# Writing the order of four engines by hand ahead of the FFN, and loading projection weights from one queue

## The chip, the cores and the metric

One Trainium2 chip, one core. The metric is the device time in microseconds of one execution of the whole program. A core has five engines that each run their own list of instructions in order: TensorE (PE in the profile: matmuls and transposes; PEld is its weight load), VectorE (DVE), ScalarE (ACT), GpSimd (POOL) and SyncE (SP, which only issues transfers). They wait for each other through semaphores. An instruction that waits holds everything behind it in its own list.

## The reference

One layer of a hybrid encoder for 2048 prompt tokens and 8 x 16 sample tokens, model width 1024, all float32:

```python
n = rmsnorm(x, norm1_g)
z, xbc, dt_raw, q, k, v, f_raw = split_columns(n @ w_in)     # 3088 columns
y_ssd = ssd_mixer(z, causal_dwconv(xbc) ... )                # 8 heads, state 128, conv width 4
y_fox = fox_prompt / fox_sample(q, k, v, logf)               # 8 heads, width 64, forget gates
h = x + concat([y_ssd, y_fox]) @ w_out
y = h + (silu(g) * v) @ w_down,  g, v = causal_dwconv(rmsnorm(h, norm2_g) @ w_up)
```

The final RMSNorm of y is an output, and so are the keys, values, log gates, SSD state and the last rows of both convolutions. The sample tokens attend to 512 cached rows and start from given states.

## The kernel before

Tokens lie in 17 tiles of 128 (16 of the prompt, tile 16 holds the sample tokens). Each float32 operand of a large matmul is split into a high half, rounded to the fast float32 format, and a low half, what is left; a product is three matmuls (`split`, `split2`).

Ahead of the FFN the program has three kinds of work.

- **Projection.** The prompt is taken in four parts of 512 tokens (`NPART`). `a_head(p)` loads the part's inputs transposed (`xT`) and by rows (`xt`), forms the row norms from squares, turns each scale into a diagonal matrix (`dg`), spreads it over the partitions by a matmul with ones, multiplies, and splits the result into `nT`. `a_body(p)` then multiplies by the weights: `proj_tm` with tokens on the partitions (v, gates, z; two halves of a weight tile each), `proj_cm` with columns on the partitions (q, k and the convolution channels). Weights are loaded as `craw` (2 buffers) and split by ScalarE (line 109) and GpSimd (line 112) into `cmw` (3 buffers, `WA`). Consumers of the results are `use_qk`, `use_v`, `use_z` and `use_x`, the last being the convolution: a scaling on ScalarE, three multiply-adds on VectorE, a tanh on ScalarE, a product on VectorE. `gates` computes gate values and cumulative sums.
- **SSD.** `ssd_chunk(c)`, one per tile: loads `xb`, `zt` and the broadcast decay sums `sg`, forms decays with ScalarE, and ends in a transposed tile stored to `mix_d`.
- **Attention.** For each part and head `s_phase` finds row maxima (VectorE, line 671) and `t_phase` forms transposed scores, exponentials `pr` on ScalarE (line 733) and the product with v (`pv`, line 696) two steps later. `sample_attention` does the cached streams.

A loop at the end interleaves them: for each attention step (`u`) it gives out a share of the side work (`sides`: sample attention in part 0, SSD chunks after) and of the filling projection (`fill`, where each piece of a generator says by a credit about how long TensorE takes). Stage 4 of the filling is the output projection: `out_weights` loads and splits `wo`, `out_proj(c)` loads a tile of `mix_d` as `raw`, splits it into `mx` (lines 102, 105) and multiplies.

What sets the order: the loop runs under a manual schedule for TensorE alone, so TensorE's list is the program's order. The lists of VectorE, ScalarE, GpSimd and SyncE are chosen by a planner, which puts instructions where its estimate of their durations has them ready. `DQ = "sass"` says which queue issues a transfer: `dma`, `dS` and `dA` SyncE, `dW` (weights) ScalarE. The FFN follows under the planner: 22 blocks of `up` and `down` in three parts.

## Time and profile before

| | |
|---|---|
| median of 3 runs | 3159.74 us (3157.91 to 3166.94) |
| profiled execution | 3159.18 us, span 3157.5 us |
| TensorE busy | 3039.0 us, 96% of the span |
| VectorE, ScalarE, GpSimd busy | 1788.8, 1066.7, 865.8 us |
| TensorE busy, 0 to 1550 us | 1445.69 us |
| TensorE busy, 1550 to 3157 us (FFN) | 1593.35 us |
| mean granted TensorE clock | 0.984 over the span, 0.97 in 0 to 1550 us |

The span is the profiled execution from its first to its last instruction. In the rows that follow, a stretch of time shows busy microseconds and the number of instructions of each engine, then the granted clock, the mean busy share of the DMA engines and their GB/s; in a timeline row the numbers are the start, the duration, the engine, the line and the operation, and in brackets how long the engine sat idle before it and what it waited for. A matmul that waits for an exponential may wait because ScalarE is held by something else in its list, so the row of the instruction ahead of it has to be read as well.

### The profile page before, as it was taken

The numbers are of one execution on the slowest core, as the hardware profiler recorded it, in microseconds if no ns is written. First come the engines' busy times: TensorE is split into PE (matmuls) and PEld (weight loads), VectorE is DVE, ScalarE is ACT, GpSimd is POOL, SyncE is SP. The second block draws the span as 40 slices with busy tenths as digits, with TensorE's granted clock in tenths as the row PEclk, the third lists the DMA queues.
The fourth block names the chain that finished last, engine by engine and source line by source line (L and its number), as shares of the span: only waits on it lengthen the run. The fifth ranks groups of instructions, "written<-read, shape, count | busy, mean of one in ns | idle before, by whom it ended". The sixth has DMA issues, their size and how long they took to land.

```text
span 3157.5 us, 45849 instructions
## 1 busy us (share of the span) xinstructions
PE 3039.0 (96%) x17888; PEld 2682.1 (85%) x17888; DVE 1788.8 (57%) x3294; ACT 1066.7 (34%) x1927; POOL 865.8 (27%) x654
## 2 busy tenths in 40 slices
PE   7988998899999998999999999999999999999998
PEld 7886877787788775777899999999999999999998
DVE  4264466647565654543455555566555556766666
ACT  3343344444444444332322232233222223332322
POOL 3322322222222212000233232333223232433332
PEclk9998999899999999999999999999999999999999
DMA  4856675575556546445522121232121122322221
GB/s 123 247 174 202 200 244 158 181 223 165 162 155 204 153 132 187 161 148 181 171 67 67 54 69 61 72 116 79 61 67 61 60 67 83 105 67 81 74 69 65
DMA packets 233137, 395.77 MB, mean 125 GB/s; under 512 B 62544, under 2 KB 118488, under 8 KB 232920
## 3 DMA queue, kind: packets, MB, share of 16 engines
q1 hardware_dynamic: 181224, 238.41, 24.3%
q10 hardware_dynamic: 51696, 154.43, 15.8%
q8 instruction: 141, 2.31, 0.3%
q14 instruction: 76, 0.62, 0.1%
HBM read 314.51 MB, written 78.25 MB: 124 GB/s over the span
## 4 chain that ended last, share of the span: by engine, by line
PE 85%; DMA 8%; DVE 2%; ACT 2%; issue 1%; SPq 1%; POOL 1%; ACTq 0%; DVEq 0%; POOLq 0%
PE mm L120 11%; PE mm L121 11%; PE mm L122 11%; PE pv L696 6%; PE dn L1025 5%; PE dn L1026 5%; PE dn L1027 5%; PE mm L444 3%; PE mm L445 3%; PE mm L446 3%; DMA xt<-in_xr 2%; PE dn L923 2%; PE dn L925 2%; PE dn L924 2%; PE mm L397 2%; PE mm L399 2%
## 5 line engine op out<-in xcount | busy, mean ns | idle before, releaser
L105 POOL TENSOR_TENSOR wr<-raw,wr 128x1024 fp32r<-128x1024 f32 x198 | 476.5, 2415 | 1032.5 <-ACT wr L102 1024.5
L120 PE MATMUL mm<-nT,wr 128*128 128x386 f32 (+1 forms) x2112 | 696.4, 330 | 1.3 <-ACT wr L102 0.8
L121 PE MATMUL mm<-nT,wr 128*128 128x386 f32 (+1 forms) x2112 | 695.3, 329 | 0.1
L122 PE MATMUL mm<-nT,wr 128*128 128x386 f32 (+1 forms) x2112 | 694.4, 329 | 0.0
L1003 DVE SCALAR_TENSOR_TENSOR ac<-mm,cw,ac 128x384 f32<-128x384 f32 (+1 forms) x528 | 301.6, 571 | 344.8 <-ACT ac L1001 337.1
L1001 ACT ACTIVATE ac<-mm,cw 128x384 f32<-128x384 f32 (+1 forms) x264 | 172.7, 654 | 784.6 <-PE mm L122 784.0
L1028 DVE TENSOR_TENSOR y<-y,dn 128x512 f32<-128x512 f32 x374 | 255.0, 684 | 267.4 <-PE dn L1027 264.6
L121 PEld LDWEIGHTS mm<-nT,wr 128*128 128x128 f32 x2112 | 399.3, 189 | 6.8 <-DVE nT L105 0.3
L120 PEld LDWEIGHTS mm<-nT,wr 128*128 128x128 f32 x2112 | 397.5, 188 | 7.7 <-ACT wr L102 1.1
L122 PEld LDWEIGHTS mm<-nT,wr 128*128 128x128 f32 x2112 | 397.9, 188 | 5.7
L112 POOL TENSOR_TENSOR cmw<-craw,cmw 128x512 fp32r<-128x512 f32 (+1 forms) x192 | 248.6, 1317 | 467.8 <-ACT cmw L109 348.1
L444 PE MATMUL mm<-nT,cmw 128*128 128x256 f32 (+2 forms) x1024 | 309.7, 302 | 12.7 <-DVE cac L489 8.6
L671 DVE TENSOR_REDUCE nm<-s 128x1 f32<-128x512 f32 (+2 forms) x320 | 192.9, 607 | 198.6 <-PE s L668 114.1
L445 PE MATMUL mm<-nT,cmw 128*128 128x256 f32 (+2 forms) x1024 | 299.0, 292 | 0.0
L446 PE MATMUL mm<-nT,cmw 128*128 128x256 f32 (+2 forms) x1024 | 299.0, 292 | 0.0
L1025 PE MATMUL dn<-wr,ht 128*128 128x512 f32 x748 | 294.4, 394 | 2.9 <-DVE y L1028 1.7
L696 PE MATMUL pv<-pr,v 128*128 128x512 f32 (+3 forms) x640 | 293.5, 549 | 0.5 <-issue 0.5
L1026 PE MATMUL dn<-wr,ht 128*128 128x512 f32 x748 | 292.7, 391 | 0.0
L1027 PE MATMUL dn<-wr,ht 128*128 128x512 f32 x748 | 290.1, 391 | 0.0
L102 ACT CAST wr<-raw 128x1024 fp32r<-128x1024 f32 x198 | 203.2, 1042 | 174.1 <-PE dn L1027 161.4
L733 ACT ACTIVATE pr<-s 128x512 f32<-128x512 f32 (+1 forms) x320 | 169.3, 531 | 237.3 <-PE s L729 173.2
L668 PE MATMUL s<-ks,q 68*128 68x512 f32 (+2 forms) x320 | 199.8, 630 | 20.0 <-ACT pr L733 11.2
(294 smaller groups left out, 5174.9 us busy)
## 6 DMA issues: line engine op xcount, KB each, us to landing
raw<-in_w_up ACTq DMA_DIRECT2D x132, 512.0 KB
raw<-in_w_down ACTq DMA_DIRECT2D x66, 512.0 KB
craw<-in_w_cm ACTq DMA_DIRECT2D x64, 512.0 KB
k<-k_d SPq DMA_DIRECT2D x80, 256.0 KB
craw<-in_w_tm ACTq DMA_DIRECT2D x24, 512.0 KB
q_d<-qk SPq DMA_DIRECT2D x96, 128.0 KB
k_d<-qk SPq DMA_DIRECT2D x96, 128.0 KB
ks<-k_d SPq DMA_DIRECT2D x80, 136.0 KB
```

What stands on the lines that cost most here:

```text
L105: leng.tensor_sub(lo, src, hi.bitcast(F32))
L120: T.matmul(ps[:, :W], whi(k), wt[:, 0, k, :W], start=k == 0, stop=False)
L121: T.matmul(ps[:, :W], whi(k), wt[:, 1, k, :W], start=False, stop=False)
L122: T.matmul(ps[:, :W], wlo(k), wt[:, 0, k, :W], start=False, stop=k == n - 1)
L444: T.matmul(ps[:, :W], wc[:, 0, k, :], wk[:, 0], start=k == 0, stop=False)
L445: T.matmul(ps[:, :W], wc[:, 0, k, :], wk[:, 1], start=False, stop=False)
L446: T.matmul(ps[:, :W], wc[:, 1, k, :], wk[:, 0], start=False, stop=k == KT - 1)
L696: m = T.matmul(pv[:, of:512], vr[:, jj], pr[:, :512 - of], start=first, stop=last)
L1003: V.scalar_tensor_tensor(ac[:, 0:n], ps[:, j:j + n], cw2[:, ct, j:j + 1], ac[:, 0:n], op0=ALU.mult, op1=ALU.add)
L1025: T.matmul(ps, ht[:, 0, ts_], wd[:, 0, cc], start=x == 0, stop=False)
L1026: T.matmul(ps, ht[:, 0, ts_], wd[:, 1, cc], start=False, stop=False)
L1027: T.matmul(ps, ht[:, 1, ts_], wd[:, 0, cc], start=False, stop=x == len(g) - 1)
```

## The change

Between the start of the attention loop's program and the FFN, the manual schedule now covers TensorE, VectorE, ScalarE and GpSimd: each runs in the order in which the program writes its instructions. SyncE keeps the planner, and so does what is written ahead of that block (the first two steps of the first head) and the FFN. With that:

- Weight tiles of the projection come from one list, `queue_of_weights`; `wload` issues from SyncE, `wsplit` splits, and `pump`, called after every piece of projection, splits the next tile when one of the three buffers is free and keeps up to two loaded. The order of projections changes: convolution tiles alternate with z, and q of the first pair stands ahead of v's first half.
- In `a_head`, the row squares are spread out, one per two pieces, each load one step ahead of its use; for the first part the diagonals go to VectorE, the low halves too, and squares lie in `k12` buffers.
- `gates`, `ssd_chunk` and `sample_attention` get more steps between a load and its use, and `sides` gives chunks out differently (7 to 15 in the last part).
- `out_weights` splits both halves on GpSimd and no longer waits for the last exponential; `out_rows` loads a tile of mixed rows ahead of the projection before it and splits it inside.

The core of the diff:

```diff
-            sq = at([P, 2, 4, 256], "cmw", WA)
+            sq = []
             for kk in range(2):
-                S.activation(sq[:, kk, :, :n * P], xTs[kk][:, :, :n * P], AF.Square)
+                sq.append(bt_([P, 4 * 264], "k12", KB)[:, 0:D].rearrange("p (k t) -> p k t", k=4))
+                S.activation(sq[kk][:, :, :n * P], xTs[kk][:, :, :n * P], AF.Square)
...
                 dg = at([P, P], "dg", 2)
-                S.activation(dg, ident, AF.Identity, scale=x)
+                if first:
+                    V.tensor_scalar_mul(dg, ident, x)
+                else:
+                    S.activation(dg, ident, AF.Identity, scale=x)
...
                 split(xT[:, :, :N], wt[:, 0, kk:kk + 4, col:col + N], wt[:, 1, kk:kk + 4, col:col + N], S,
-                      V if kk else G)
+                      V if kk or first else G)
...
         xTs = load(*todo[0])
-        ss = [sizes(todo[0][2] + c) for c in range(4)]
-        yield
+        xt = half_row(0)
+        yield
+        ss = []
+        for n in range(8):
+            if n % 2 == 0:
+                x = at([P, 2], "ss", 4)
+            S.activation(xt, xt, AF.Square, accum_out=x[:, n % 2:n % 2 + 1])
+            if n < 7:
+                xt = half_row(n + 1)
+            if n % 2:
+                V.tensor_add(x[:, 0:1], x[:, 0:1], x[:, 1:2])
+                rsq(x[:, 0:1], D)
+                ss.append(x[:, 0:1])
+            yield
...
+    def wload():
+        src, n = wq[len(raws)]
+        raw = at([P, 4 * 272], "craw", 2)
+        raw = raw[:, 0:D].rearrange("p (k c) -> p k c", c=P) if n is None else raw[:, 0:4 * n].rearrange("p (k c) -> p k c", c=n)
+        dma(raw, src.rearrange("p (k c) -> p k c", c=P) if n is None else src)
+        raws.append(raw)
+
+    def wsplit():
+        j = len(tiles)
+        n = wq[j][1]
+        if n is None:
+            we = at([P, 2, KT, P], "cmw", WA, F32R)
+        else:
+            we = at([P, 2, 4, n], "cmw", WA, F32R)
+        split2(raws[j], we[:, 0], we[:, 1], G)
+        tiles.append(we)
+
+    def pump():
+
+        if len(tiles) < len(raws) and len(tiles) - used[0] < WA:
+            wsplit()
+        while len(raws) < len(wq) and len(raws) - len(tiles) < 2:
+            wload()
...
-        for ct in range(8):
-            yield from proj_cm(8 + ct, use_x(ct), PAD1)
-        yield from proj_tm(i["w_tm"][1], 256, use_z(0))
-        yield from proj_tm(i["w_tm"][2], 256, use_z(1))
+        yield from proj_cm(use_x(0), PAD1)
+        yield from proj_tm(256, use_z(0))
+        yield from proj_cm(use_x(1), PAD1)
+        yield from proj_tm(256, use_z(1))
+        for ct in range(2, 8):
+            yield from proj_cm(use_x(ct), PAD1)
...
         dma(sg.rearrange("p h l -> p (h l)"), ac_d[c:c + 1].rearrange("c h p -> c (h p)").to_broadcast([P, D]))
+        yield
+        yield
...
             w = op.tile([P, 2, D], F32R, tag="wo", name="wo", bufs=KT)
-            with tc.issue_after(exps[-1]):
-                split2(raws[k], w[:, 0], w[:, 1], G)
+            split(raws[k], w[:, 0], w[:, 1], G, G)
...
+    def out_rows(c):
+
         mr = op.tile([P, KT, P], F32, tag="raw", name="raw", bufs=2)
+
+        parts = [slice(0, KT - 1), slice(KT - 1, KT)] if 12 <= c < 16 else [slice(0, KT)]
+        for ks in parts:
+            dA(mr[:, ks], mix_d[c][:, ks])
+        yield
         mx = op.tile([P, 2, KT, P], F32R, tag="mx", name="mx", bufs=2)
-
-        for ks in ([slice(0, KT - 1), slice(KT - 1, KT)] if 12 <= c < 16 else [slice(0, KT)]):
-            dA(mr[:, ks], mix_d[c][:, ks])
+        for ks in parts:
             split(mr[:, ks], mx[:, 0, ks], mx[:, 1, ks], S, V)
+        yield mx
...
-            if k in (12, 40) and hd:
+            if hd and (k >= 8 and k % 2 == 0 and k <= 24 or k == 40):
                 next(hd)
...
-    sides = {0: (sample_attention, 5 * NB + 1), 1: (lambda: chunks(SMP, 0, 1, 2), 49), 2: (lambda: chunks(3, 4, 5, 6, 7), 51),
-             3: (lambda: chunks(*range(8, 16)), 81)}
-
-    with tc.manual_schedule(engines={nc.tensor.engine}):
+    sides = {0: (sample_attention, 6 * NB + 1), 1: (lambda: chunks(SMP, 0, 1), 45), 2: (lambda: chunks(2, 3, 4, 5, 6), 61),
+             3: (lambda: chunks(*range(7, 16)), 109)}
+
+    with tc.manual_schedule(engines={e.engine for e in (T, V, S, G)}):
```

Three places show what moves. First, ScalarE's list near the end of part 0's q and k projections and the start of the convolution. `xt` are the half rows that are squared for the next part, `cac` and `cth` the convolution before and in its tanh, `ev` is evicted z or v, `craw` and `cmw` are the raw and split weights. Before:

```order
L197 ACTIVATE xt,ss<-xt 128x512
L487 ACTIVATE cac<-mm,cw_169 128x384
L109 CAST cmw<-craw 128x1024
L197 ACTIVATE xt,ss<-xt 128x512
L487 ACTIVATE cac<-mm,cw_169 128x256
L432 DMA craw<-in_w_cm 128x1024
L497 ACTIVATE cth<-cac 128x384
L197 ACTIVATE xt,ss<-xt 128x512
L497 ACTIVATE cth<-cac 128x256
```

And with the change:

```order
L484 ACTIVATE ev<-mm 128x256
L259 ACTIVATE xt,ss<-xt 128x512
L109 CAST cmw<-craw 128x1024
L541 ACTIVATE cac<-mm,cw_182 128x256
L551 ACTIVATE cth<-cac 128x256
L109 CAST cmw<-craw 128x1024
L803 ACTIVATE pr<-s 128x512
L259 ACTIVATE xt,ss<-xt 128x512
L541 ACTIVATE cac<-mm,cw_182 128x384
L551 ACTIVATE cth<-cac 128x384
```

The squares now stand mostly among z's evictions, the weight load has left the list, and each tanh follows its scaling directly, where before another instruction stood between.

Second, ScalarE's list where the output projection begins under attention (`wo` the output weights, `mx` a tile of mixed rows, `sg` a chunk's decays, `pr` exponentials). Before:

```order
L109 CAST wo<-raw 128x1024
L733 ACTIVATE pr<-s 128x512 x3
L109 CAST wo<-raw 128x1024
L102 CAST mx<-raw 128x1024
L733 ACTIVATE pr<-s 128x512 x2
L532 ACTIVATE sg<-sg,acs 128x128 x8
L102 CAST mx<-raw 128x1024
L533 ACTIVATE sg<-sg 128x1024
```

And with the change:

```order
L803 ACTIVATE pr<-s 128x512 x2
L602 ACTIVATE sg<-sg,acs 128x128 x8
L603 ACTIVATE sg<-sg 128x1024
L803 ACTIVATE pr<-s 128x512 x2
L612 COPY bs<-s 128x256
L803 ACTIVATE pr<-s 128x512 x2
L102 CAST mx<-raw 128x1024 x2
L803 ACTIVATE pr<-s 128x512
```

The casts of `wo` are gone from ScalarE (GpSimd has them), and the exponentials no longer stand behind them.

Third, SyncE's list in part 0, around the first z tiles of the change (`xb_d` and `z_d` are stores of the convolution and of z, `ks` a load for attention). With the change:

```order
L421 DMA craw<-in_w_tm 128x1024
L554 DMA xb_d<-cth 128x2x128
L699 DMA ks<-k_d 68x512
L554 DMA xb_d<-cth 128x2x128
L556 DMA xb_d<-cth 128x128
L487 DMA z_d<-ev 128x256 x2
L421 DMA craw<-in_w_tm 128x1024
L195 DMA xt<-in_xr 128x512
```

Before, no `craw` stood in this list: the loads were ScalarE's, as in the first piece above. Now they stand between stores that wait for ScalarE's and VectorE's results.

More of the change, by code (lines that the diff above doesn't have):

```diff
@@ L185, in sizes_by_columns @@
                 for k in range(KT):
-                    T.matmul(pz[:, c:c + 1], sq[:, k // 4, k % 4, c * P:(c + 1) * P], ones[:, 0:1], start=k == 0, stop=k == KT - 1)
+                    T.matmul(pz[:, c:c + 1], sq[k // 4][:, k % 4, c * P:(c + 1) * P], ones[:, 0:1], start=k == 0, stop=k == KT - 1)
             ss = at([P, 2], "ss", 4)
@@ L403, in proj_tm @@
                     yield 1.45
+            used[0] += 2
         dtf = at([P, 5, 16], "dtf", 1)
@@ L423, in use_z, with proj_cm @@
             return f
-        yield from proj_tm(i["w_tm0"], 272, use_v(1))
-        gs = gates(p, dtf)
-        next(gs)
-        yield from proj_tm(i["w_tm"][0], 256, use_v(0))
-        def load_cm(ct):
-            raw = at([P, 4 * 272], "craw", 2)
-            dW(raw[:, 0:D], i["w_cm"][ct])
-            wc = at([P, 2, KT, P], "cmw", WA, F32R)
-            split2(raw[:, 0:D].rearrange("p (k c) -> p k c", c=P), wc[:, 0], wc[:, 1], G)
-            return wc
-        def proj_cm(ct, use, pad):
-            wc = load_cm(ct)
+        def proj_cm(use, pad):
+            wc, = need(1)
             for w, wt in wins:
@@ L450, in proj_cm @@
                 yield W * 0.0055
+            used[0] += 1
         def use_qk(kind, pair):
@@ L887, in hybrid_step @@
     tp = op = pso = None
-    wo = []
+    wo, ready = [], []
     def out_weights():
@@ L937, in out_proj @@
                             yield 1.36
+                        if e and k == 4 and nxt is not None:
+                            ready.append(next(nxt))
         for e in range(2):
@@ L1201, in out_steps @@
         yield from out_weights()
-        for c in [SMP] + list(range(11)):
-            yield from out_proj(c)
+        cs = [SMP] + list(range(11))
+        g = out_rows(cs[0])
+        next(g)
+        yield ("wait", 3)
+        mx = next(g)
+        for n, c in enumerate(cs):
+            g = out_rows(cs[n + 1]) if n + 1 < len(cs) else None
+            if g:
+                next(g)
+            yield from out_proj(c, None, mx, g)
+            mx = ready.pop() if g else None
     F = ExitStack()
```

82 lines of the change are left out of this document (59 added, 23 removed).

## The prediction

> **What bounds the kernel now.** I read the table by stretches first (length, busy time of each engine, granted TensorE clock, DMA share), cut where the work changes: head, projections alone, four stretches of attention mixed with projections and SSD chunks, output projection under attention, FFN.
>
> ```profile
> 0.00:50.00 50.00, 30.77 (x153) 29.77 (x154) 22.61 (x67) 17.37 (x24) 19.74 (x28) 0.97 0.37 118
> 50.00:160.00 110.00, 102.45 (x725) 99.06 (x725) 39.57 (x118) 33.98 (x80) 35.19 (x31) 1.00 0.72 218
> 160.00:480.00 320.00, 285.28 (x2240) 244.82 (x2239) 169.01 (x438) 120.83 (x265) 87.75 (x84) 0.92 0.65 200
> 480.00:800.00 320.00, 303.96 (x2046) 254.02 (x2046) 199.91 (x398) 136.71 (x295) 87.91 (x92) 0.97 0.61 183
> 800.00:1180.00 380.00, 368.44 (x2382) 296.42 (x2380) 222.05 (x422) 163.30 (x343) 91.97 (x100) 0.99 0.54 162
> 1180.00:1250.00 70.00, 55.14 (x259) 36.87 (x260) 35.76 (x57) 32.80 (x64) 25.79 (x28) 0.88 0.66 194
> 1250.00:1550.00 300.00, 299.66 (x1406) 226.32 (x1405) 134.60 (x206) 92.85 (x189) 19.57 (x43) 1.00 0.48 164
> 1550.00:3157.00 1607.00, 1593.35 (x8689) 1494.83 (x8687) 965.26 (x1589) 468.81 (x669) 497.89 (x250) 1.00 0.23 74
> ```
>
> TensorE sets the time; the FFN (1607 us) is full and untouched. Ahead of it TensorE idles 19.2 + 7.6 + 34.7 + 16.0 + 11.6 + 14.9 + 0.3 = 104.3 us. Length times (1 - clock) adds 1.5 + 25.6 + 9.6 + 3.8 + 8.4 = 48.9 us of withheld clock. No other engine is over two thirds busy in a stretch. So the prize is small gaps, and the next views say what ends them: TensorE's waits, then ScalarE's, both for 0 to 1550 us (total, times, longest).
>
> ```profile
> PE s L570 <- ACT pr L733: 12.6, 2, 9.1
> PE s L668 <- ACT pr L733: 11.2, 6, 5.1
> PE mm L444 <- DVE cac L489: 8.6, 3, 5.0
> PE s L588 <- DVE ss L198: 7.8, 1, 7.8
> ACT xt L197 <- DMA xt<-in_xr: 64.7, 21, 6.3
> ACT mx L102 <- PE dn L925: 60.8, 15, 9.8
> ACT cth L497 <- DVE cac L489: 39.2, 31, 4.0
> ACT sg L532 <- DMA sg<-ac_d: 35.0, 14, 5.7
> ```
>
> TensorE waits for softmax exponentials (pr) that are not slow themselves: they stand in ScalarE's queue behind an instruction that waits for a transfer (xt, sg, mx). The timeline of ScalarE and TensorE shows the largest such gap:
>
> ```profile
> 1230.82 1.04 ACT L109 CAST wo<-raw 128x1024 fp32r<-128x1024 f32 x1 [6.43 <-DMA raw<-in_w_out]
> 1236.57 1.04 ACT L102 CAST mx<-raw 128x1024 fp32r<-128x1024 f32 x1 [4.71 <-DMA raw<-mix_d]
> 1237.52 1.08 ACT L733 ACTIVATE pr<-s 128x512 f32<-128x512 f32 x2
> 1238.16 2.08 PE L570 MATMUL s<-sst,xb 128*128 128x256 f32 x4 [9.06 <-ACT pr L733]
> ```
>
> **The change, part by part.** The matmuls stay the same in number and kind; only waits can move.
>
> Head. The row-norm diagonals move from ScalarE to VectorE, and both low halves of the first windows go to VectorE.
>
> ```profile
> 16.77 0.71 POOL L189 TENSOR_TENSOR ss<-ss,mhalf 128x2 f32<-128x2 f32 x1 [1.53 <-DVE ss L188]
> 19.56 0.69 ACT L206 ACTIVATE dg<-ident,ss 128x128 f32<-128x128 f32 x2 [1.17 <-DMA q_d<-q]
> 20.02 1.22 PE L225 MATMUL tp<-dg,ones 128*128 128x128 f32 x4 [5.79 <-ACT dg L206]
> 26.49 0.59 PE L399 MATMUL mm<-cmw,nT 128*128 128x272 f32 x1 [1.61 <-POOL nT L105]
> ```
>
> The scale is ready at 17.48 and ScalarE takes it at 19.56; VectorE can take it at once: 2 us. Two more diagonals follow later; with the GpSimd wait I take -3 us (0 to -5).
>
> Weight loads: 96 leave ScalarE's queue for SP's. ScalarE loses issue time that is on no path. Where TensorE has only projections (50 to 160 us) the 12 constant-row stores now fall too, since their fill is in VectorE's program order; before, SP did them in the head:
>
> ```profile
> 10.17 6.52 SPq L1162 DMA_DIRECT2D q_d<-q  x8
> 17.11 6.89 SPq L1162 DMA_DIRECT2D k_d<-q  x4
> ```
>
> That is 13.8 us of SP's queue, ahead of the v stores that free the eviction buffers. Three buffers and three PSUM tiles stand between; I take 0, with bounds -4 (half of the 7.6 us idle) and +10.
>
> Squares of the next part's rows (24 of xt). They were bunched, each load issued once the square before it was done; now they are two projection steps apart, with the load issued a step ahead. Stretch 160:480 holds the first eight and the sample attention, whose caches are now loaded a step ahead too. Of its 34.7 us idle I take half, -17, because the two projection steps there are short against a load and some waits stay (bounds 0 and -28).
>
> Stretch 480:800. The one long gap is VectorE's bunch, in its timeline, with TensorE's row behind it:
>
> ```profile
> 544.08 3.39 DVE L713 RECIPROCAL rdb<-rdb 128x128 f32<-128x128 f32 x4 [0.76 <-ACT rdb L710]
> 550.21 3.09 DVE L229 SCALAR_TENSOR_TENSOR xT<-xT,g1c,tp 128x256 f32<-128x256 f32 x8
> 553.22 2.55 DVE L717 TENSOR_TENSOR yl<-yl,rdb 128x512 f32<-128x512 f32 x1
> 557.13 2.07 PE L588 MATMUL s<-k,cm 128*128 128x256 f32 x4 [7.85 <-DVE ss L198]
> ```
>
> In written order one reciprocal goes to each attention step and the four multiplies stand apart: -8 of 16.0 (bounds 0, -13). Stretch 800:1180: chunk loads get two more steps before use, which is the sg wait: -5 of 11.6 (0 to -9).
>
> Stretch 1180:1250. Output weights are split wholly on GpSimd, so ScalarE no longer waits for them, and the mixed rows are loaded a tile ahead.
>
> ```profile
> L112 POOL TENSOR_TENSOR wo<-raw,wo 128x512 fp32r<-128x512 f32 x16 | 20.2, 1282 | 24.8 <-ACT wo L109 24.3 <-DMA k<-k_d 0.4
> L109 ACT CAST wo<-raw 128x1024 fp32r<-128x1024 f32 x8 | 8.3, 1040 | 13.7 <-DMA raw<-in_w_out 13.7
> ```
>
> GpSimd's cast of such a tile has no row: between ScalarE's 1.04 us and GpSimd's own subtraction, 2.56; I take 2.56, the same engine. Eight add 20.5 us to 25.8 busy of 70, so it fits; the v fills and the chunk norms queue behind up to 5 us. -11 of 14.9 (-5 to -13).
>
> Idle removed: 3 + 17 + 8 + 5 + 11 = 44 us.
>
> Clock. The withheld time goes with the gaps in its stretch: 25.6 x 17/34.7 + 9.6 x 8/16 + 3.8 x 5/11.6 + 8.4 x 11/14.9 = 25 us. TensorE was not busy all through a slow slice:
>
> ```profile
> 280.00:300.00 20.00, 13.93 (x81) 8.15 (x84) 8.01 (x23) 8.67 (x21) 2.93 (x4) 0.67 0.59 185
> 860.00:880.00 20.00, 19.77 (x116) 15.88 (x115) 13.38 (x23) 7.86 (x15) 3.02 (x3) 0.92 0.47 155
> 858.96 0.50 PE L729 MATMUL s<-q,k 68*128 68x512 f32 x1 [2.43 <-DVE q L686]
> ```
>
> 13.93 of 20 is 0.70, so -17 us (0 to -34).
>
> The Trainium skill ("TensorE: Matmul & The Clock Gate", Part 1) says that the clock halves after an idle window of about 3.4 us and is full again after as long a busy one. The second and third rows do not bear out a single gap as the condition: the clock fell to 0.92 right after a gap of 2.43 us. By the page, with every longer gap gone, all the clock returns; that is the first rival.
>
> New cost. In the convolution the order now is ScalarE's scale, three VectorE steps, ScalarE's tanh, with nothing between.
>
> ```profile
> L489 DVE SCALAR_TENSOR_TENSOR cac<-mm,cw,cac 128x256 f32<-128x256 f32 x192 | 91.8, 479 | 60.9 <-ACT cac L487 58.3
> ```
>
> ScalarE is held 3 x 0.479 = 1.44 us in each of 64 windows, 92 us, against 39 now: +53 us of hold. Today 8.6 of those 39 us reach TensorE, a share of 0.22: +12 us (0 to +53).
>
> **Sum.** -44 - 17 + 12 = -49. From the profiled execution's own 3159.2 us (span 3157.5; the median of the runs, 3159.7, is the same) this gives **3110 us**. Its own range: half of what is removed, -30 + 12, gives 3141; gaps nearly gone, 65 of idle and 25 of clock with no new cost, gives 3069.
>
> **Rivals.**
>
> First, the clock pays in full: the gaps that are left are too short or too few to slow it. -44 - 0.70 x 48.9 + 12 = -66, 3093 us. For it: 1250:1550 runs at 1.00 with 0.3 us idle. Against: the 2.43 us gap above.
>
> Second, the conv hold reaches TensorE whole: -44 - 17 + 53 = -8, 3151 us, within the noise. For it: VectorE is 60% busy in 480:800, so three steps rarely start at once. Against: exponentials are used two attention steps after they are issued.
>
> Third, slower: SP is now the only queue for weights, and its order is still the planner's. A load behind a store waits for that store's data.
>
> ```profile
> 236.45 13.05 SPq L422 DMA_DIRECT2D z_d<-ev  x5
> 177.91 5.03 DMA craw<-in_w_cm
> L109 ACT CAST cmw<-craw 128x1024 fp32r<-128x1024 f32 (+1 forms) x96 | 100.1, 1044 | 18.0 <-PE mm L399 18.0
> L112 POOL TENSOR_TENSOR cmw<-craw,cmw 128x512 fp32r<-128x512 f32 (+1 forms) x192 | 248.6, 1317 | 467.8 <-ACT cmw L109 348.1 <-issue 34.5 <-DMA k<-k_d 21.2
> ```
>
> Five z stores held SP for 13 us. A load caught behind them, 13 late, lands after 5 and is split in 1.0 + 2.6; a tile lasts 1120 / 96 = 11.7 us (96 loads by about 1120 us), so some 10 us reach TensorE. Five such loads undo the gain; ten, spread over the four parts, make it 3159 - 49 + 100 = 3210 us. For it: stores of z and of the convolution are interleaved tile by tile with the loads. Against: the ring keeps two raw and three split tiles, and ScalarE's own queue, where loads stood till now, was held as long by xt and mx.
>
> The Trainium skill ("DMA: Bandwidth & Descriptors", section "Issuing engines are not separate DMA queues") says that all issuers share the same 16 DMA engines, so a second one saves only issue time. By it the move costs nothing; it leaves out that a waiting store holds its queue, as the 13.05 us row shows.
>
> **Chances.** Forecast 0.55, first rival 0.13, second 0.12, third 0.20. The likeliest case alone spans 3069 to 3141 us. For 8 in 10 I take 3062 to 3185: below are a few hundredths of the first case and rival one, above about two thirds of the third. A measurement here tells 0.3%, 9.5 us. Faster: 0.55 + 0.13 + a little of the second = 0.69; same 0.10; slower 0.21.
>
> **What will show it.** Right: in 160:480 TensorE busy by 300 of 320 us at the same work and clock at 0.96 or more; no exponential behind mx, wo or sg; xt's 64.7 us down by more than half; the FFN stretch unchanged at 1607 us. Wrong: matmuls of the projections waiting for a cmw split whose load left SP late (third), ScalarE's tanh waits over 90 us with TensorE behind them (second), or a head longer than 50 us to the same matmul. The forecast fails if the idle ahead of the FFN stays above 85 us.

## The result, and the profile after

The change makes the kernel slower: 3231.39 us (median of 4 runs, 3228.09 to 3234.06) against 3161.38 us (3157.91 to 3166.94), a ratio of 1.0228 with a 95% interval of 1.0213 to 1.0243. The forecast was 3110 us; the third rival had the sign but, as will be seen, not the cause.

The profiled execution has a span of 3227.8 us against 3157.5. TensorE's busy time grew from 3039.0 to 3065.5 us at the same 17888 matmuls: 26.5 us. That goes with a lower granted clock, 0.976 over the span against 0.984. Its idle time (span less busy) grew from 118.5 to 162.3 us: 43.8. Together 70.3, the whole difference.

The first view is the table by stretches of the kernel after, cut where the prediction cut it, with the stretch before the FFN (at 1627 us now) apart; three rows between 1180 and 1627 us are left out. Columns: window, length, busy time of TensorE, its weight loads, VectorE, ScalarE and GpSimd with their instructions, granted clock, DMA share, GB/s.

```profile
0.00:50.00 50.00, 30.07 (x134) 29.06 (x135) 20.85 (x54) 14.45 (x16) 11.87 (x20) 0.90 0.34 117
50.00:160.00 110.00, 93.64 (x634) 91.85 (x634) 27.87 (x92) 26.68 (x60) 27.94 (x22) 0.89 0.58 170
160.00:480.00 320.00, 269.77 (x2054) 232.10 (x2052) 142.49 (x412) 102.59 (x220) 76.68 (x74) 0.90 0.60 181
480.00:800.00 320.00, 294.53 (x1955) 244.70 (x1955) 182.45 (x377) 125.94 (x271) 86.81 (x89) 0.95 0.62 183
800.00:1180.00 380.00, 365.09 (x2373) 293.55 (x2372) 225.08 (x430) 168.16 (x357) 101.88 (x111) 0.99 0.58 168
...
1627.00:3228.00 1601.00, 1588.07 (x8666) 1490.63 (x8665) 964.38 (x1587) 466.44 (x667) 495.77 (x249) 1.00 0.23 73
```

The FFN takes 1601 us as it did. All is lost ahead of it, and by the clock column mostly before 480 us: the stretch from 50 to 160 us had a clock of 1.00 and has 0.89.

Since the work in a fixed window differs between the two kernels, the timelines were also lined up by work: the start of the n-th first score matmul of the attention (line 728 before, 798 after; 320 of them in each). This table is counted from TensorE's timeline; the four kernels at the right are experiments that follow.

| attention step | before | after | TensorE alone | VectorE free | spaced | spaced, VectorE free |
|---|---|---|---|---|---|---|
| 0 | 168.2 | 184.1 | 178.0 | 172.7 | 188.1 | 173.8 |
| 8 | 261.5 | 282.6 | 260.5 | 260.3 | 282.7 | 257.7 |
| 24 | 413.6 | 452.1 | 413.3 | 408.8 | 444.6 | 406.4 |
| 32 | 454.1 | 510.7 | 467.2 | 467.5 | 498.0 | 458.1 |
| 64 | 608.7 | 667.5 | 615.5 | 624.9 | 655.6 | 609.1 |
| 128 | 846.4 | 900.9 | 848.3 | 860.1 | 881.8 | 836.1 |
| 248 | 1223.1 | 1290.3 | 1238.4 | 1237.8 | 1266.3 | 1211.7 |
| 256 | 1269.5 | 1326.4 | 1274.7 | 1272.1 | 1304.7 | 1246.0 |
| 319 (last) | 1461.2 | 1521.1 | 1471.5 | 1466.8 | 1499.0 | 1441.0 |

After minus before is +15.9 us when attention begins, +56.6 at step 32, and about that at the last step (+59.9). Most of the loss is made in the first part: head, gates, and the sample attention among the first part's projections. From there to the last step the change loses and gains about as much: 10.6 us lost from step 32 to 248, 10.3 gained from 248 to 256. The remaining 10.4 of the 70.3 us come between the last step and the FFN, where TensorE has one hole of 4.18 us up to 1550.21 (it waits for VectorE's addition into y, line 1023) and a clock of 0.97 against 1.00; a part of that stretch is work that stood ahead of the last step before.

Two holes of TensorE show how. The first is in the stretch with projections alone. These rows are from the timelines of SyncE, VectorE and TensorE after, with other rows between them left out:

```profile
72.00 8.04 SPq L1245 DMA_DIRECT2D q_d<-q  x8
80.09 5.25 SPq L1245 DMA_DIRECT2D k_d<-q  x4
91.90 0.27 SPq L355 DMA_DIRECT2D k_d<-g_2k  x1
80.76 0.68 DVE L354 COPY g_2k<-tp 8x512 f32<-8x512 f32 x1 [0.55 <-PE tp L352]
94.66 0.68 DVE L354 COPY g_2k<-tp 8x512 f32<-8x512 f32 x1 [13.22 <-DMA k_d<-g_2k]
95.26 0.20 DVE L361 TENSOR_TENSOR g_dm<-g_ld,blkb 128x64 f32<-128x64 f32 x1
95.61 0.66 PE L363 MATMUL tp<-g_dm,ones 128*128 128x64 f32 x2 [13.05 <-DVE g_dm L361]
```

VectorE has filled a one-buffer row (g_2k) at 81.4 us and must fill it again. The store that frees it is issued by SyncE at 91.90 only, behind the twelve constant rows and what piled up behind them. VectorE stands, and g_dm, a 0.20 us product whose inputs were there at 70.8 us, stands behind it in the list; TensorE waits 13.05 us for that product, and its clock is 0.62 from 80 to 100 us.

The second is at the end of the first part:

```profile
429.30 0.40 SPq L788 DMA_DIRECT2D mix_d<-yl  x1
434.06 0.58 ACT L779 COPY yl<-pv 64x512 f32<-64x512 f32 x1 [12.30 <-DMA mix_d<-yl]
436.32 0.16 DVE L925 TENSOR_TENSOR snm<-snm 128x1 f32<-128x1 f32 x1 [12.94 <-ACT pr L924]
437.01 0.42 DVE L515 SCALAR_TENSOR_TENSOR qk<-mm,qk 128x256 fp32r<-128x256 f32 x1
437.90 0.59 PE L497 MATMUL mm<-nT,cmw 128*128 128x260 f32 x1 [8.98 <-ACT ev L518]
```

A late store holds ScalarE's copy of yl; the sample attention's exponentials (pr, line 924) stand behind that copy; VectorE's sum of them (snm) waits 12.94 us; the eviction of a projection (qk, line 515) stands behind the sum; the eviction of ScalarE behind it frees the PSUM tile for which TensorE waits 8.98 us. ScalarE, VectorE and TensorE each stood at the head of their list for the one before.

### The profile page after: what moved, and what is told of

Same layout as the page of the kernel before. It is cut to its first block, busy times and chain, and to the rows that moved or that the text cites. A ratio compares the mean times of both kernels' runs of the same rounds, so it can differ in the third digit from the quotient of the medians.

```text
span 3227.8 us, 45891 instructions
## 1 busy us (share of the span) xinstructions
PE 3065.5 (95%) x17888; PEld 2696.5 (84%) x17888; DVE 1784.4 (55%) x3302; ACT 1056.0 (33%) x1914; POOL 863.3 (27%) x651
## 3 DMA queue, kind: packets, MB, share of 16 engines
q10 hardware_dynamic: 28656, 103.83, 10.3%
## 4 chain that ended last, share of the span: by engine, by line
PE 77%; DVE 5%; DMA 5%; ACT 2%; issue 2%; SPq 1%; POOL 0%; DVEq 0%; ACTq 0%; POOLq 0%
PE mm L120 11%; PE mm L121 11%; PE mm L122 11%; PE pv L766 5%; PE dn L1108 5%; PE dn L1109 5%; PE dn L1110 5%; PE mm L497 2%; PE mm L499 2%; PE mm L498 2%; PE dn L1004 2%; PE dn L1006 2%; PE dn L1005 2%; PE s L799 1%; PE s L798 1%
```

## The experiments

Two theories at the start. **Q**: SyncE, now the only queue for the weights, is late with loads and stores. **O**: VectorE, ScalarE and GpSimd in written order stand still at the head of their lists, where the planner had put other work ahead. The runs were made in five rounds, and the median of the kernel before moved between 3156.32 and 3162.40 us from round to round, so a few microseconds between runs tell nothing; each ratio is to the kernel before in the same round.

**TensorE alone by hand** (`te_only`)

```diff
-    with tc.manual_schedule(engines={e.engine for e in (T, V, S, G)}):
+    with tc.manual_schedule(engines={nc.tensor.engine}):
```

> The order of ahead-of-FFN work is kept by hand for TensorE alone; ScalarE, VectorE and GpSimd go back to the planner's order, and everything else of the change (loads, stores, queues) stays. Theory Q (one queue: weight loads, constant rows and late stores on one list make the loss): the loss stays, 3210 to 3230 us. Theory O (order: ScalarE, VectorE and GpSimd stand still at the head of a hand-written list, where the planner put other work ahead): the loss goes, 3165 us or less.

Measured: 3177.89 us (3172.93 to 3180.18), ratio 1.0056 (1.0037 to 1.0076). With the loads, stores and queues of the change in place, 53 of 70 us are gone: O carries most, though not all that it promised (3165). The rest, some 16 us, is the cost of everything else in the change; 10 us of it are there at the start of the attention.

**Constant rows early** (`const_early`)

```diff
+    constant_rows()
     with tc.manual_schedule(engines={e.engine for e in (T, V, S, G)}):
...
-            if k == 12:
-                constant_rows()
```

> The constant rows' stores are issued in the head, before the hand-written order begins. Theory Q: the 13.05 us hole of TensorE at 82.56 goes, and with it the cold clock behind it, so 15 to 20 us less than the change, about 3213. Theory O: under 8 us less, because another wait of the list takes its place, about 3225.

Measured: 3233.6 us, ratio 1.0231 (1.0201 to 1.0260). No gain, and both numbers for it were off. From ScalarE's and TensorE's timelines of that run:

```profile
28.64 1.06 ACT L183 ACTIVATE k<-qk 128x1024 f32<-128x1024 f32 x1 [18.13 <-DMA qk<-in_xTw]
33.01 0.59 PE L461 MATMUL mm<-cmw,nT 128*128 128x272 f32 x1 [14.69 <-ACT nT L102]
98.62 0.66 PE L363 MATMUL tp<-g_dm,ones 128*128 128x64 f32 x2 [4.95 <-DVE g_dm L361]
```

The hole did shrink, from 13.05 to 4.95 us, and a new one of 14.69 us stands in the head (2.83 us there in the change): SyncE issues the second window's load at 22.92, behind the rows, ScalarE stands 18.13 us for it, and the split of the first window (nT), for which TensorE waits, stands behind that in ScalarE's list. It moved.

**Weights from ScalarE's queue** (`act_queue`, and `te_only_act_queue` with TensorE alone by hand)

```diff
-        dma(raw, src.rearrange("p (k c) -> p k c", c=P) if n is None else src)
+        dW(raw, src.rearrange("p (k c) -> p k c", c=P) if n is None else src)
```

> The projection weights are issued from ScalarE's queue instead of SP's; the order is that of the change. Theory Q: SP's list is shorter by all weight loads, at least 30 us less than the change, 3200 or less. Theory O: within 10 us of 3231, the weights were there in time on either queue.

Measured: 3345.07 us, ratio 1.0583 (1.0553 to 1.0614). Neither theory had this: 114 us more. ScalarE's timeline of the run, beside one load:

```profile
278.93 1.03 ACT L109 CAST cmw<-craw 128x1024 fp32r<-128x1024 f32 x1
282.60 0.33 ACTq L421 DMA_DIRECT2D craw<-in_w_tm  x1
282.98 0.56 ACT L541 ACTIVATE cac<-mm,cw 128x256 f32<-128x256 f32 x1 [3.03 <-POOL cmw L112]
```

The load needs the buffer that ScalarE has just cast at 278.93 and that GpSimd's subtraction still reads. In written order ScalarE waits for that, 3 us here, before it can issue, and the convolution behind it waits too. So the issue of a load is an instruction with a wait, and it holds what is behind it. Counted over the whole timeline, ScalarE stands idle for 284 us directly ahead of the 96 issues here, and for 75 us in `te_only_act_queue`, where the planner orders its list. The Trainium skill ("DMA: Bandwidth & Descriptors", section "Issuing engines are not separate DMA queues") says that issuing from several engines at once saves the issue time alone; here the choice of the engine was worth 114 us in one order of the list and under 8 in the other:

> TensorE alone in written order (3178 us), and the weight loads issued from ScalarE's queue as before the change, instead of SP's. If SP as the only queue costs by itself (my third rival), at least 8 us come back, 3170 or less. If not, 3174 to 3184; with all four by hand the same edit cost 114 us, which would then belong to ScalarE's written order.

Measured: 3170.35 us (3168.48 to 3171.98), ratio 1.0030 (1.0014 to 1.0046), where `te_only` had 1.0056 (1.0037 to 1.0076). The intervals overlap; it is 7 us lower by the medians, at the edge of what was expected of Q, and about a tenth of the loss at the most.

**A buffer for the late store** (`yl_apart`) and **the sums later** (`sums_later`) each take one link out of the second hole's chain.

```diff
-            vn = bt_([NT, 512], "yl", 2)
+            vn = bt_([NT, 512], "xe", 1)
```

> The sample attention's v rows are held in another buffer (that of xe), so that the copy into yl on ScalarE does not wait for SP's store of the v rows. If ScalarE's 12.30 us and 7 us holds by that store are on the path, attention steps 0 to 32 take 10 to 15 us less than in the change, about 3218. If the gates on VectorE or the conv's tanh are late next, the time stays within 4 us of 3231.

```diff
-            V.tensor_add(nm[:, 5:6], nm[:, 3:4], nm[:, 4:5])
-            V.reciprocal(nm[:, 5:6], nm[:, 5:6])
-            V.tensor_scalar_mul(nm[:, 6:8], par, nm[:, 5:6])
             yield
...
             V.tensor_copy(pt5, pk[0:NT, 0:P])
             yield
+            V.tensor_add(nm[:, 5:6], nm[:, 3:4], nm[:, 4:5])
+            V.reciprocal(nm[:, 5:6], nm[:, 5:6])
+            V.tensor_scalar_mul(nm[:, 6:8], par, nm[:, 5:6])
```

> The change, with one thing moved: in the sample attention VectorE's three small steps on the exponentials' sums stand two pieces later in its list, behind the transposes' copy, so that VectorE no longer waits there for ScalarE's exponentials (26.7 us in 8 waits between 180 and 520 us in the change, longest 12.9). Theory V (VectorE's list, held by ScalarE's results, is what costs in the first part): attention steps 0 to 32 get 8 to 15 us shorter, 3216 to 3223 us. If the hold comes from the projection's evictions instead: within 5 us of 3231.

Measured: 3226.24 us, ratio 1.0207 (1.0178 to 1.0237), and 3233.02 us, ratio 1.0231 (1.0201 to 1.0261). The first took the 8.98 us hole away and was 8 us ahead of the change at step 24, of which 4 were left at step 40: 5 us at the end by the medians, half of what I expected, and the intervals of the two overlap, so a gain in time is not shown. The second gave nothing, and the timeline of VectorE says why:

```profile
437.62 0.42 DVE L515 SCALAR_TENSOR_TENSOR qk<-mm,qk 128x256 fp32r<-128x256 f32 x1 [13.64 <-ACT qk L514]
```

The next instruction of the list took the wait over: it reads ScalarE's result too, and ScalarE stood as long as ever (12.73 us for yl).

**Where and on which engine** (`hand_late`, `vector_free`, `scalar_free`)

```diff
-    with tc.manual_schedule(engines={e.engine for e in (T, V, S, G)}):
+    with tc.manual_schedule(engines={e.engine for e in (T,)}):              # hand_late: to step 40, then all four
+    with tc.manual_schedule(engines={e.engine for e in (T, S, G)}):         # vector_free
+    with tc.manual_schedule(engines={e.engine for e in (T, V, G)}):         # scalar_free
```

> TensorE alone in written order up to attention step 40 (projection of the first part and the sample attention), all four engines in written order from there to the FFN. With all four by hand 69 us were lost, with TensorE alone 16. Theory O1: the other engines' written order costs only in the first part, where sample attention, projection and gates meet; then 3175 to 3185 us. Rival O2: it costs wherever it is used, and what came late in the first part only covers it later; then 3200 us or more.

> TensorE, ScalarE and GpSimd in written order, VectorE by the planner. If VectorE's list is what holds the others (the convolution's steps, the gates, the row maxima), most of the 53 us between the change and TensorE alone returns: 3195 us or less. If ScalarE's list is it (exponentials behind tanh, copies and scalings that wait), it stays above 3215 us.

> TensorE, VectorE and GpSimd in written order, ScalarE by the planner. TensorE's gaps in the change end mostly on ScalarE (exponentials pr), so if ScalarE's list is the cause, 3195 us or less; if VectorE's list holds what ScalarE waits for, above 3215 us. If neither this nor the run with VectorE free falls under 3200, the two hold each other.

Measured:

| | us | ratio to before |
|---|---|---|
| hand_late | 3181.57 (3179.68 to 3185.46) | 1.0066 (1.0043 to 1.0089) |
| vector_free | 3168.97 (3161.57 to 3173.21) | 1.0027 (1.0013 to 1.0041) |
| scalar_free | 3251.30 (3250.72 to 3251.88) | 1.0279 (1.0249 to 1.0309) |

So O1 holds by the times: with four engines by hand from step 40 on, no difference from TensorE alone can be told (1.0066 against 1.0056). The two profiles also reach the last step together (1472.2 and 1471.5 us); only from there to the FFN's first matmul does `hand_late` take longer, 103.4 us against 97.3. That stretch takes 103 to 104 us in the change, `spaced` and `scalar_free` too, and 97 to 98 in `vector_free` and `spaced_vector_free`, so some 6 us are lost there wherever VectorE is by hand. And the order that costs most is VectorE's: with it alone given back to the planner 62 us return. Giving back ScalarE's alone makes it 20 us slower still, the one result of the three that I had no account of beforehand: ScalarE's list then differs, but what it reads still comes from VectorE in written order.

What the planner does with VectorE shows at the first hole. From SyncE's and VectorE's timelines of `vector_free` (the first and the last row of the constant rows' twelve stores, then VectorE; rows between are left out):

```profile
10.04 3.68 SPq L1245 DMA_DIRECT2D q_d<-q  x6
24.76 1.01 SPq L1245 DMA_DIRECT2D k_d<-q  x1
68.11 0.22 DVE L361 TENSOR_TENSOR g_dm<-g_ld,blkb 128x64 f32<-128x64 f32 x1
75.27 0.68 DVE L354 COPY g_2k<-tp 8x512 f32<-8x512 f32 x1 [1.56 <-PE tp L352]
78.89 0.67 DVE L354 COPY g_2k<-tp 8x512 f32<-8x512 f32 x1
```

The fill of the constant rows is an instruction of VectorE; the planner pulls it into the head, so the stores fall at 10 to 26 us, where before they fell at 10 to 24. And it takes g_dm at 68.11, 10.8 us ahead of the second copy of g_2k behind which it was written.

**Each step behind the result it reads** (`spaced`, and `spaced_vector_free` with VectorE by the planner). The projections' evictions become generators that a list holds; each goes one step on at every half piece of projection:

```diff
                 S.activation(ac[:, :off], ps[:, PAD1:W], AF.Identity, scale=cw1[:, ct, 3:4], bias=cw1[:, ct, 4:5])
-                for j in range(3):
-                    V.scalar_tensor_tensor(ac[:, 0:n], ...)
-                S.activation(th[:, :off], ac[:, :off], AF.Tanh)
-                V.scalar_tensor_tensor(th[:, :off], ...)
+                def g():
+                    for j in range(3):
+                        V.scalar_tensor_tensor(ac[:, 0:n], ...)
+                    yield False
+                    S.activation(th[:, :off], ac[:, :off], AF.Tanh)
+                    yield False
+                    V.scalar_tensor_tensor(th[:, :off], ...)
+                    yield True
+                owed.append(g())
```

The same for the second step of z and of q and k; the sums stand as in `sums_later`.

> The same, and in the projection's evictions (q and k, z, convolution) each engine's step stands half a projection piece or more behind the step of the other engine whose result it reads; all four engines are still in written order. Theory V: the waits of VectorE and ScalarE on each other (33.7, 27.2, 26.7, 17.6 us on VectorE; 20.6 and 18.3 on ScalarE between 180 and 520 us) go, and with them half or more of the 62 us between the change and VectorE by the planner: 3200 us or less. If written order as such costs (each list waits for something else next): above 3215 us.

> The same spacing, VectorE by the planner, the others in written order: 3169 us without the spacing. My prediction took 12 us of TensorE's time (0 to 53) for ScalarE's hold by the convolution's tanh. If that holds, 3150 to 3160 us; if the hold reaches TensorE whole, 3120 to 3140; if it reaches nothing, 3165 to 3172.

Measured: `spaced` 3204.82 us, ratio 1.0142 (1.0112 to 1.0171); `spaced_vector_free` 3144.22 us (3142.49 to 3145.36), ratio 0.9958 (0.9936 to 0.9981). By the medians, the spacing gives 27 us beside VectorE's written order (5 us short of what theory V asked) and 25 beside a free VectorE: the two add. The 3144 us lie between the two ranges that I gave for that run, and the kernel is faster than both that were compared, than the one before by 0.4%, with an interval that ends below 1. Its table by stretches, cut at the start of the attention, step 32, the last step and the FFN, and below it that of before, cut at the same work:

```profile
0.00:174.00 174.00, 146.91 (x956) 143.85 (x957) 64.80 (x193) 49.10 (x96) 45.72 (x49) 0.94 0.57 171
174.00:458.00 284.00, 254.71 (x2021) 217.61 (x2021) 150.53 (x395) 101.90 (x223) 80.74 (x77) 0.92 0.67 205
458.00:1441.00 983.00, 952.94 (x5798) 750.54 (x5797) 569.23 (x1065) 408.61 (x881) 234.74 (x264) 0.98 0.58 172
1441.00:1540.00 99.00, 98.22 (x454) 80.56 (x453) 43.95 (x64) 25.82 (x50) 7.70 (x14) 1.00 0.64 216
```

```profile
0.00:168.00 168.00, 141.22 (x930) 136.44 (x931) 66.49 (x199) 55.27 (x111) 58.21 (x62) 0.99 0.61 186
168.00:454.00 286.00, 256.46 (x2049) 218.98 (x2048) 151.02 (x402) 106.07 (x233) 78.27 (x75) 0.92 0.67 206
454.00:1461.00 1007.00, 959.02 (x5813) 758.56 (x5813) 568.33 (x1050) 413.98 (x868) 225.77 (x255) 0.97 0.55 167
1461.00:1556.00 95.00, 94.22 (x437) 77.40 (x436) 38.97 (x59) 24.88 (x49) 8.23 (x14) 1.00 0.57 204
```

Head and end still lose 6 and 4 us; the third row gains 24, 18 of it idle (48.0 to 30.1) and 6 busy. That is the size of the gain that the prediction looked for from 480 to 1250 us, once VectorE's list is the planner's and the evictions are spaced. In the stretch from which it took most, 160 to 480 us, the second row gains 2.

**Is it ScalarE's and GpSimd's written order that gains there?** (`spaced_te_only`, `spaced_te_act_queue`: the spacing with TensorE alone by hand, weights from SyncE or ScalarE)

> The spacing with TensorE alone in written order; VectorE, ScalarE and GpSimd by the planner. Without the spacing this was 3178 us, and with the spacing and VectorE alone free 3144. If the planner undoes or has no need of the spacing: 3168 to 3178. If the spacing is worth as much here as beside a free VectorE (25 us): 3150 to 3156, and ScalarE and GpSimd in written order are a gain of some 10 us.

> The same with the weights issued from ScalarE's queue: 7 us less than the run before it, if what that move gave without the spacing adds up; nothing, if the spacing already relieves SP's late stores.

Measured: 3173.21 us, ratio 1.0051 (1.0030 to 1.0072), and 3171.64 us, ratio 1.0051 (1.0031 to 1.0071). The planner has no use for the spacing (1.0056 without it), and the weights' queue makes no difference here. Against 0.9958 with ScalarE and GpSimd by hand, their written order gains about 29 us; without the spacing it gained about 9 (1.0027 against 1.0056). The two engines were not tried apart. The waits of ScalarE up to 1550 us, first with TensorE alone by hand, then with ScalarE and GpSimd too (total, times, longest), show some that went; the wait for sg has no row in the second. Which of them reached TensorE is not shown:

```profile
ACT xt L259 <- DMA xt<-in_xr: 63.1, 20, 8.6
ACT mx L102 <- PE dn L1035: 57.7, 11, 11.8
ACT sg L631 <- DMA sg<-ac_d: 50.7, 14, 7.9
```

```profile
ACT xt L259 <- DMA xt<-in_xr: 38.1, 13, 8.7
ACT mx L102 <- PE dn L1035: 35.9, 4, 9.8
```

**The hole at 82 us, twice more** (`spaced_gate_buffer`, `spaced_rows_gpsimd`; and both with the spacing and VectorE free, `vector_free_gate_buffer`, `vector_free_rows_gpsimd`)

```diff
-            fr = at([8, 512], "g_2k", 1)
+            fr = at([P, 512], "xt", XB)[0:8] if a and p == 0 else at([8, 512], "g_2k", 1)   # gate_buffer
...
-                dma(row.rearrange("h r k -> r h k") ...
+                nc.gpsimd.dma_start(row.rearrange("h r k -> r h k") ...                      # rows_gpsimd
```

> All four engines in written order with the spacing (3205 us), and the second of the two rows that the gates store to k_d gets a buffer of its own in the first part, so that VectorE's second copy no longer waits for SP's store of the first (TensorE's hole of 16.25 us at 82). If the hole is VectorE's list standing behind one late store: 12 to 22 us less, clock included, 3183 to 3193. If another store on SP is late next and holds the same place: 3198 or more.

> All four engines in written order with the spacing (3205 us); the twelve constant rows' stores are issued by GpSimd instead of SP, at the same place of the program. SP's 13.6 us block ahead of the gates' stores is gone. If VectorE's hole at 82 (16.25 us, the wait for the store to k_d) is that block, the hole falls under 6 us and the time to 3180 to 3193. If GpSimd's weight splits behind its own issues are late next: 3200 or more.

> The spacing and the gates' own buffer, VectorE by the planner, ScalarE and GpSimd in written order: 3144 us without the buffer. The planner already put other work ahead of the second copy, so at most the 3.96 us hole at 81 goes: 3136 to 3144.

> The same, VectorE by the planner (3144 us with the rows on SP): the planner moves the memset and the rows, and no hole over 5 us is left there, so at most a few us: 3136 to 3144; 3148 or more if GpSimd's issues delay its splits.

Measured:

| | us | ratio to before |
|---|---|---|
| spaced_gate_buffer | 3207.76 | 1.0165 (1.0145 to 1.0186) |
| spaced_rows_gpsimd | 3209.66 | 1.0156 (1.0118 to 1.0194) |
| vector_free_gate_buffer | 3143.74 (3139.82 to 3150.82) | 0.9958 (0.9942 to 0.9975) |
| vector_free_rows_gpsimd | 3155.39 (3148.78 to 3160.58) | 0.9982 (0.9967 to 0.9996) |

Neither closes the hole. With the buffer, VectorE's next writer of that buffer took the wait over, 15.57 us for the same late store. With the rows on GpSimd, the 13.8 us in which SyncE issued them in `spaced` are off its list, and SyncE is late all the same. Its timeline and GpSimd's:

```profile
75.61 6.23 SPq L549 DMA_DIRECT2D q_d<-qk  x1
81.89 3.67 SPq L550 DMA_DIRECT2D q_d<-qk  x1
85.61 2.23 SPq L551 DMA_DIRECT2D q_d<-qk  x1
87.94 2.40 SPq L488 DMA_DIRECT2D out_v<-ev  x1
92.60 0.30 SPq L355 DMA_DIRECT2D k_d<-g_2k  x1
...
72.40 4.67 POOL L1274 DMA_DIRECT2D q_d<-q  x8 [3.75 <-DVE q L1270]
77.07 0.56 POOL L1274 DMA_DIRECT2D k_d<-q  x1
84.92 1.68 POOL L1274 DMA_DIRECT2D k_d<-q  x3 [7.28 <-DMA q_d<-q]
```

While the rows are in flight, single issues on SyncE take 1.6 to 6.2 us, where those of the same lines took 0.4 to 0.9 in `spaced`, and GpSimd itself stands 7.28 us between two of its own. So at this place the twelve stores hold SyncE about as long whoever issues them. In the head, beside VectorE's written order, they cost as much (`const_early`); fewer of them was not tried.

With VectorE free the buffer changes nothing. The rows on GpSimd give back over half of the gain by the ratios (0.9982 against 0.9958), though the intervals overlap. They fall at 66 to 78 us there, not in the head as I expected, and where `spaced_vector_free` has a hole of 3.96 us TensorE now waits 14.36:

```profile
95.15 1.10 PE L383 MATMUL tp<-ident,g_2k 128*128 128x128 f32 x4 [14.36 <-DVE g_2k L104]
```

These two runs also part the rows from the rest of VectorE's order. With the rows on GpSimd, at 72 to 87 us with VectorE by hand and at 66 to 78 without, VectorE by the planner is still worth 54 us (3209.66 against 3155.39), so most of what its written order costs is not the place of the rows.

**The output part alone** (`before_out_rows`): the kernel before, with `out_weights`, `out_rows` and `out_proj` of the change.

```diff
-            with tc.issue_after(exps[-1]):
-                split2(raws[k], w[:, 0], w[:, 1], G)
+            split(raws[k], w[:, 0], w[:, 1], G, G)
```

> The kernel before with one part of the change: output weights split on GpSimd, rows of the output projection loaded a tile ahead and split within the tile before. My prediction took 11 us of idle and most of 8 us of clock from stretch 1180 to 1250: then 3143 to 3150 us. If the gap only moves (the split on GpSimd delays v and the chunks), 3155 to 3165.

Measured: 3159.98 us, ratio 1.0000 (0.9983 to 1.0017). The gap of 9.06 us moved. From TensorE's and ScalarE's timelines:

```profile
1193.73 2.08 PE L696 MATMUL pv<-pr,v 128*128 128x512 f32 x2 [7.33 <-ACT pr L733]
1234.48 0.79 PE L728 MATMUL s<-q,k 128*128 128x512 f32 x1 [7.56 <-ACT pr L733]
1191.34 1.86 ACT L532 ACTIVATE sg<-sg,acs 128x128 f32<-128x128 f32 x6 [10.83 <-DMA sg<-ac_d]
1230.40 2.45 ACT L532 ACTIVATE sg<-sg,acs 128x128 f32<-128x128 f32 x8 [8.92 <-DMA sg<-ac_d]
```

ScalarE now stands behind the chunks' sg load instead of behind the output weights, and TensorE has two holes of over 7 us for it.

## Why the prediction was wrong, step by step

- **What bounds the kernel** was read rightly: FFN untouched (1601 us in both), all of the difference ahead of it in TensorE's idle time and clock. It was made the other way.
- **The sum had no term for the new order itself.** It costed waits that the written order removes, and one that it adds (the convolution). The price of VectorE's written order was left out, which puts it at nothing. Measured: 62 us between the change and `vector_free`. That is the step that failed. Of the waits that I removed by moving a load a step ahead, the largest (xt) shrank as said; the planner's order had gone around others, which showed in no row of before because nothing waited there.
- **Stretch 50 to 160, "0, bounds -4 and +10".** The 13.8 us of constant-row stores were seen, with their move into this stretch. I looked for their victim among the v stores and counted three buffers; the victim was the gates' one-buffer row and VectorE's list behind it: 13.05 us of idle in one hole and a clock of 0.62 from 80 to 100 us. Attention starts 15.9 us late, head included. Head: the diagonals' wait fell from 5.79 us to 4.16, and TensorE waits 6.19 us from 38 us on for the squares of the sample rows (line 183).
- **Stretch 160 to 480, "-17".** The named wait did shrink (`xt`, 64.7 to 23.3 us in the first row below, against "down by more than half"); the attention steps 0 to 32, in which it lies, take 40.7 us more, by chains of the kind of the second hole.
- **Stretches 480 to 1180, "-13".** Steps 32 to 248 go from 769.0 to 779.6 us: no gain. With VectorE free and the evictions apart they take 753.6, -15, near the forecast; with VectorE free alone 770.3, no gain. So the size could be had, but by the spacing, which the change did not have; that it came from the waits I named is not shown.
- **Stretch 1180 to 1250, "-11".** Steps 248 to 256 fell from 46.4 to 36.1 us, -10 and as said. But not for the reason given: the output part alone leaves the time as it was, since ScalarE then waits for sg. It takes more of the change, the chunks' extra steps or their new distribution, which were not run alone. The 2.56 us that I gave to GpSimd's cast of an output weight tile were 1.06 in the change.
- **Clock, "-17".** It is +26.5 us of busy time. It went with the gaps, as said: idle time grew too, by 43.8 us. The clock column is an average of full and half clock: the trace's clock records hold 1.0 and 0.5 alone. The 0.92 of the prediction's slice is 3.4 us at 0.51, from 859.8 on, behind the gap of 2.43 us. In the change a gap of 2.42 us that ended at 70.88 was followed by 6.8 us at 0.50, from 71.1 on, with TensorE busy all through; so gaps far shorter than the two holes cost clock too.
- **Convolution hold, "92 us of ScalarE, +12".** The size of the hold was right:

```profile
ACT xt L259 <- DMA xt<-in_xr: 23.3, 10, 6.2
ACT cth L551 <- DVE cac L543: 96.4, 55, 3.2
```

  Whether +12 was its price stays open. Spacing it apart, together with z, q and k, gives 25 to 27 us, inside the bounds of 0 and +53; what of that is the tanh's was not measured alone.
- **Third rival, slower by late weight loads.** Right in sign, and in that a store ahead on SyncE holds what is behind it. But no projection matmul waits for a weight tile in TensorE's waits up to 1550 us, and the loads' queue is worth 7 us with TensorE alone by hand and nothing with the spacing. What the stores held was VectorE's and ScalarE's lists, by buffers not yet free.
- **First and second rival.** The clock could not pay in full, since the gaps grew. Of the second's sign half came: the tanh's waits are over 90 us, but no projection matmul waits for the convolution's multiply-adds ahead of the FFN, where 8.6 us of such waits stood before. Whether the hold reached TensorE by exponentials behind the tanh is not shown.
- **The conditions named.** Of the signs of being right, xt's wait and the FFN's time came. These came out as failures: idle ahead of the FFN "above 85 us" (149 us up to 1550 us), a head longer than before, a clock of 0.90 in 160 to 480.

What stays open: which instructions of VectorE's list make up the rest of the 60 us between `spaced` and `spaced_vector_free`. The table of steps shows 14 of them at step 0, 26 more by step 32 and 18 from there to the last step, and 5 come behind it; single links taken out gave 5 us or nothing. Open too is why ScalarE by the planner beside VectorE by hand is slower than both by hand.

## What to carry to other kernels

Writing an engine's order by hand takes away the planner's freedom to go around a late wait. Price it by asking, for every instruction that waits in the new list, what is written behind it. Here it paid where each instruction stood a step behind the result it reads: ScalarE and GpSimd by hand gained about 29 us with the evictions spaced and about 9 without. VectorE by hand lost some 60 either way; that a second buffer or an earlier store would have made it pay is not shown, since the runs that gave it one moved the wait. So do it one engine at a time and measure each. When one link of a chain of such waits is taken out and the time stays, look at the next instruction of the same list before blaming another cause.

## What the runs showed of the hardware that was not expected

- The place where a transfer is issued is a wait in that engine's list: 96 loads moved to ScalarE cost 114 us when its list was in written order and nothing, or a gain of some 7 us, when it was planned.
- Issues on one engine slowed down while another engine's stores were in flight: 1.6 to 6.2 us each on SyncE against 0.4 to 0.9, during GpSimd's twelve stores of 32 KB, and up to 4.5 us in `vector_free_rows_gpsimd`.
- The Trainium skill ("PSUM — Partial Sum Buffer", section "Engine vs sequencer instructions") says that the lists of ScalarE, VectorE and GpSimd are strictly first in, first out. The trace of the change agrees at the first hole: a product of 0.20 us stood behind a copy that it had nothing to do with while that copy waited 13.22 us.
